# Folding the Fourier branch of an encoder block onto the symmetric half of its rows and columns

## The chip, the core and the metric

The kernel runs on one core of one Trainium2 chip. The metric is device microseconds (us) of one execution. The core has a matrix engine (TensorE, in the profile PE, its weight loads PEld), VectorE (DVE), ScalarE (ACT) and GpSimd (POOL). SyncE (SP) issues most DMA transfers; POOL issues some. Each engine works through its own instructions in program order, and they meet by semaphores.

## What is computed

One hybrid encoder layer, applied to two inputs, `prompt` and `sample`, of 2048 rows by 1024 columns each, with the same weights. One combined projection gives attention's q, k, v and gate `ga`, and the Fourier branch's input `f` (512 columns, 8 groups of 64) and gate `gf`. Cut to what matters:

```python
def _fourier_branch(f, w_fmix):
    B, S, _ = f.shape
    fg = f.reshape(B, S, N_FGROUPS, FGROUP_DIM).astype(jnp.float32)
    ff = jnp.real(jnp.fft.fft2(fg, axes=(1, 3), norm="ortho")).astype(f.dtype)
    fm = jnp.einsum('bsgc,gcd->bsgd', ff, w_fmix)
    return fm.reshape(B, S, F_WIDTH)

def _layer(h, p, g_norm, w_in, g_q, g_k, w_fmix, w_out, g_ple, w_ple_gate, w_ple):
    u = _rmsnorm(h, g_norm)
    z = u @ w_in
    q, k, v, ga, f, gf = jnp.split(z, [int(c) for c in cuts], axis=-1)
    ...
    q = _apply_axial_rope(_rmsnorm(q, g_q), cos, sin)
    k = _apply_axial_rope(_rmsnorm(k, g_k), cos, sin)
    a = _blocked_gqa(q, k, v) * jax.nn.silu(ga)
    fo = _fourier_branch(f, w_fmix) * jax.nn.silu(gf)
    h = h + jnp.concatenate([a, fo], axis=-1) @ w_out
    gate = jax.nn.sigmoid(_rmsnorm(h, g_ple) @ w_ple_gate)
    return h + (p @ w_ple) * gate
```

The branch takes the real part of a two-dimensional Fourier transform of `f`, over all 2048 rows and over the 64 columns of each group, and then multiplies each group by its own 64x64 matrix.

## The kernel before

**Tiles.** Each input is cut into 16 tiles of 128 rows; two tiles make a chunk, so there are 16 chunks, 8 (c = 0 to 7) for each input. Matrix products keep f32 accuracy by splitting both sides into an f16 value and an f16 remainder; `SPLIT3` names the three products of four that are summed. So a product over 1024 inputs takes 24 matmuls (8 slices by 3).

**Order of rows.** `token_order` sorts the rows so that tile t holds rows t, t+16, t+32 and so on (and for t > 8 the same in reverse). The transform over 2048 rows is then a first transform inside one tile, a multiplication by phase factors, and a second transform over 16 tiles. The factors are folded into the constants `c_dft2`.

**Start.** `weights` (L293) prepares the weights of the projection block by block in the order kv, q, f, gf, ga. Each block is 8 tiles of 128 rows. A tile is loaded on SP (L304), DVE takes its largest magnitude (L312), POOL reduces that over partitions (`p_mm`, L322, a PARTITION_ALL_REDUCE), DVE makes a power of two of it (L272 to L279), and ACT and DVE write the two f16 parts (L334, L335). `load` runs ahead of the block that is worked on, as far as buffers allow.

**Projection.** `project` (L566) has an iteration for each chunk. PE makes q, k and v of the chunk (`mm_q`, `mm_kv`; all projection matmuls are recorded at L451), then the sweep of the chunk before (`sweep_f` L915, `sweep_ga` L945): for each of two tiles 24 matmuls of 512 columns for `f` and as many for `gf`, after each gf the first transform of the tile (`first`, one f32 matmul, L925), and four times 24 matmuls of 256 columns for `ga`. POOL's queue stores the results to DRAM (`gd` L928, `gfd` L942, `agd` L960). Beside it, `norm_q` and its helpers normalise and rotate q and k (POOL L589 to L719, DVE, ACT) and transpose them by DMA on SP (L745, L748). `sweep_part(us)` interleaves a sweep by estimated microseconds with the code of the next iteration. Every fifth step of a sweep also advances a generator of background work (later weights, `channel_map`), and `ahead`, which starts the first scores of attention.

**Fourier, second part.** `fourier2` (L990) works through 16 blocks, 8 for each input. A block takes two loads of `gd` (`g_in`), 8 f32 matmuls of 128 columns (L1085), and a mix by `bd` (L1041, 8 matmuls). `bd` is made by `channel_map` (L501), kept in DRAM (`bdd`) and loaded at L1067. In the blocks with t = 0 and 8 a correction `fx` is added (L1101, L1043). From here on `attention` (L1124) sets the pace; `interleave` (L1662) puts `fourier2` and then `outp` (L1359) between its groups of scores, by estimates, with FILL the estimated length of that filler.

## Time and profile before

| what | us |
|---|---|
| median of 3 runs | 2667.2 (2664.6 to 2668.03) |
| profiled execution | 2670.38 |
| its span, first to last instruction | 2668.6 |
| PE busy | 2600.4 (97%) |
| POOL busy | 1773.2 (66%) |
| DVE busy | 1629.1 (61%) |
| ACT busy | 1186.0 (44%) |

The mean granted clock of TensorE was 0.994 of full speed. Busy time is time in which an instruction was being executed. In a row of the timeline the first number is the start, the second the length; `out<-in` names the tiles; brackets hold the idle time before and what ended it ("issue": the engine waited for nothing that the profile shows). A run of alike instructions is one row with its count (an f32 matmul leaves two records).

### The profile page before, as it was taken

Reading aid. Unit: us, or ns where it says so; the run is one execution under the profiler, and the core shown is the slowest. Engines: PE = TensorE matmul, PEld = TensorE weight load, DVE = VectorE, ACT = ScalarE, POOL = GpSimd, SP = SyncE. Lnnn points to the kernel's source line nnn. Section 1 sums busy time; section 2 is a strip of 40 time slices with the busy share of each in tenths; the row PEclk is TensorE's granted clock in tenths of the full one; section 3 lists DMA queues with packets and bytes.
Section 4 is the critical chain, followed back from the end, with each engine's and each line's share of the span. In section 5 each row is a group of like instructions: output and inputs, shape, how many; then the busy total and the mean of one; then the engine's idle time right before and its main releaser. Section 6 shows DMA issues by size and latency. Waiting matters only on the chain. (4 is left out here: it accounts for less than half of the span.)

```text
span 2668.6 us, 50160 instructions
## 1 busy us (share of the span) xinstructions
PE 2600.4 (97%) x20096; PEld 1393.3 (52%) x20096; DVE 1629.1 (61%) x2300; ACT 1186.0 (44%) x1983; POOL 1773.2 (66%) x1505
## 2 busy tenths in 40 slices
PE   6999999999999999999999999999999999999998
PEld 3565655655556654545455544444444544454443
DVE  6756465565555775566675666666665666656634
ACT  4443243433224553554444554544544544444442
POOL 1233242333336996888888888888888888888870
PEclk9999999999999999999999999999999999999999
DMA  8567576676528773222222224322232322232233
GB/s 251 146 165 199 170 210 179 174 186 153 146 67 254 232 215 85 63 66 66 74 72 62 66 62 96 101 68 72 64 87 63 76 75 75 63 84 75 64 76 73
DMA packets 453386, 305.38 MB, mean 114 GB/s; under 512 B 294272, under 2 KB 394816, under 8 KB 453152
## 3 DMA queue, kind: packets, MB, share of 16 engines
q1 hardware_dynamic: 440240, 260.41, 37.9%
q0 software_dynamic: 12912, 41.77, 4.3%
q8 instruction: 157, 2.57, 0.4%
q14 instruction: 77, 0.63, 0.1%
HBM read 149.50 MB, written 86.51 MB: 88 GB/s over the span
## 5 line engine op out<-in xcount | busy, mean ns | idle before, releaser
L1174 POOL TENSOR_TENSOR acc<-acc,p 128x1024 f32<-128x1024 f32 x384 | 934.8, 2434 | 118.2 <-ACT p L1169 86.3
L1204 DVE TENSOR_REDUCE a_mx<-ps_m 128x1 f32<-128x1024 f32 x498 | 609.0, 1223 | 544.7 <-PE ps_m L1196 535.8
L1169 ACT ACTIVATE p<-ps_s,s_scale 128x512 f32<-128x512 f32 x1024 | 648.2, 684 | 646.2 <-PE ps_s L1166 626.0
L1487 PE MATMUL ps_g<-w_pg,hT 64*128 64x512 f16 x2784 | 493.6, 377 | 2.1 <-DVE h L1413 2.1
L1232 PE MATMUL ps_o<-p,v 128*64 128x256 f32 x4096 | 468.4, 382 | 0.0
L451 PEld LDWEIGHTS <-uc 128*128 128x128 f16 x3072 | 301.5, 98 | 312.0 <-issue 20.6
L1166 PE MATMUL ps_s<-q,k 64*128 64x512 f16 x3072 | 434.1, 378 | 5.8 <-ACT p L1169 5.6
L1232 PEld LDWEIGHTS ps_o<-p,v 128*64 128x64 f32 x4096 | 283.9, 137 | 160.5 <-issue 28.5
L1487 PEld LDWEIGHTS <-hT 64*128 64x128 f16 x2784 | 205.3, 94 | 155.6 <-issue 13.8
L1487 PE MATMUL ps_g<-w_wo,mh 64*128 64x512 f16 x1440 | 260.3, 377 | 1.2 <-DVE seen L1453 1.2
L1487 PE MATMUL ps_g<-w_wo,mT 64*128 64x512 f16 x1440 | 256.2, 376 | 0.0
L1166 PEld LDWEIGHTS <-k 64*128 64x128 f16 x3072 | 151.3, 94 | 200.7 <-issue 78.0
L1196 PE MATMUL ps_m<-k,q 64*128 64x512 f16 x996 | 200.6, 378 | 11.3 <-DVE a_mx L1204 10.9
L942 POOL DMA_DIRECT2D gfd<-gt x32 | 19.7, 616 | 224.4 <-DVE gt L970 191.3
L451 PEld LDWEIGHTS <-w_ga 128*128 128x128 f16 x1536 | 148.8, 98 | 33.4 <-issue 11.1
L1172 POOL TENSOR_TENSOR acc<-p,p 128x1024 f32<-128x1024 f32 x64 | 150.9, 2358 | 20.7 <-ACT p L1169 19.8
L1487 PEld LDWEIGHTS <-mh 64*128 64x128 f16 x1440 | 100.2, 94 | 90.7 <-issue 18.3
L1487 PEld LDWEIGHTS <-mT 64*128 64x128 f16 x1440 | 102.8, 94 | 80.3 <-issue 3.8
L1255 DVE RECIPROCAL ps_f<-ps_f 128x256 f32<-128x256 f32 x63 | 110.6, 1756 | 20.5 <-PE ps_f L1248 20.5
L960 POOL DMA_DIRECT2D agd<-gat x64 | 35.5, 555 | 109.5 <-DVE gat L970 105.3
L451 PE MATMUL ps_x<-w_f,uc 128*128 128x512 f16 x480 | 105.9, 379 | 0.0
L451 PE MATMUL ps_x<-uc,w_ga 128*128 128x256 f16 x936 | 105.5, 273 | 0.0
(328 smaller groups left out, 3307.6 us busy)
## 6 DMA issues: line engine op xcount, KB each, us to landing
q<-qTd SPq DMA_DIRECT2D x256, 64.0 KB, 2.3
ag<-agd SPq DMA_DIRECT2D x64, 256.0 KB, 3.3
out<-h POOLq DMA_DIRECT2D x31, 512.0 KB, 3.1
x<-in_x_prompt SPq DMA_DIRECT2D x16, 512.0 KB, 5.1
gfd<-gt POOLq DMA_DIRECT2D x32, 256.0 KB, 2.6
gd<-ge POOLq DMA_DIRECT2D x32, 256.0 KB, 2.9
w_st<-in_w_out SPq DMA_DIRECT2D x32, 256.0 KB, 4.0
agd<-gat POOLq DMA_DIRECT2D x64, 128.0 KB, 3.1
```

The costliest lines, as they stand in the source:

```text
L451: self.nc.tensor.matmul(ps, lhs(ia, k), rhs(ib, k), start=(i == 0), stop=(i == 3 * ks - 1))
L942: lambda t=t, gt=gt: nc.gpsimd.dma_start(self.gfd[s][t], gt[:]))
L960: nc.gpsimd.dma_start(self.agd[s][1, r * 128:(r + 1) * 128, c * n:(c + 1) * n], gt[:, :n])
L1166: nc.tensor.matmul(S[u][e][:], w[sl], q[sl].rearrange("p h q -> p (h q)"), start=j == i == 0, stop=i + 1 == len(todo), skip_group_check=True)
L1169: nc.scalar.activation(p[:, e, :], S[u][e][:], AF.Exp, scale=self.sc["s_scale"][:])
L1172: nc.gpsimd.tensor_tensor(out=ACC[u][:], in0=P[u, 0][:], in1=p[:], op=ALU.add)
L1174: nc.gpsimd.tensor_tensor(out=ACC[u][:], in0=ACC[u][:], in1=p[:], op=ALU.add)
L1196: nc.tensor.matmul(ps[c], Q[u][0][sl, h, :], kt[s, kv, half][sl, :, 0, :], start=True, stop=True)
L1204: nc.vector.reduce_max(MX[u][:, h, half, c:c + 1], x, axis=AX.X)
L1232: nc.tensor.matmul(o[64 * f:64 * f + 64], vt[s, kv, c // 8][:, c % 8, :], p[:, e, f], start=(c == 0), stop=(c == 15))
L1255: nc.vector.reciprocal(r, r)
L1487: nc.tensor.matmul(g[0][:], g[1](ia, k)[sl], g[2](ib, k)[sl], start=a, stop=z, skip_group_check=True)
```

## The change

The Fourier transform of real data over rows can be made from sums and differences of row r and its mirror row 2048 - r, and over columns from column c and its mirror 64 - c. The change uses both. The mirrored columns are handled in the weights: the host reorders the 512 f columns of `w_in` into 8 x 33 = 264 "cosine" columns and 8 x 31 = 248 "sine" columns, and `fold_cols` turns the pairs into sums and differences on the chip, with three POOL operations on each of the eight loaded tiles of the block f. The mirrored rows are handled in u: `token_order` now puts tile t and tile t + 8, its mirror, into one chunk. For the chunks with c > 0, `fold_u` adds the f16 parts of u to f32 and `fold_s` makes sum and difference of the two tiles (both on POOL), and `fold_hl` splits them again (ACT and DVE). Sums meet only cosine columns, differences only sine columns, so f takes 24 pairs of 264 and 248 columns for a chunk instead of 48 matmuls of 512. One first transform, one `ft`, one `ge` and one store to `gd` then serve a chunk. The tiles of c = 0 (two chunks) mirror into themselves: their f stays as it was, and `first` uses four matmuls of 64 outputs and one more (`gx`, stored to `gxd`).

In `fourier2` a block takes one load of `gd` (block 0 of each input also `gxd`), 3 + 2 matmuls for the second transform and 3 + 2 for the mix; the order of blocks is 1 to 7, 0, 8 to 15. `channel_map` multiplies by a loaded mask (`c_mask`) in place of a memset and copies. The second half of v is loaded at group 6 of attention, since its buffers hold the first `gd` blocks until then. FILL goes from 765 to 756.

```diff
+CHB = ((0, 0, range(3)), (0, 99, range(3, 6)), (0, EVEN - 128, range(6, 8)),
+       (1, 0, range(4)), (1, 512 - EVEN - 128, range(4, 8)))
+BLOCKS = (1, 2, 3, 4, 5, 6, 7, 0) + tuple(range(8, 16))
...
+def token_order():
+    return base_order().reshape(2, NT // 2, 128).transpose(1, 0, 2).reshape(NT, 128)
...
+    def fold_cols(self, w):
+        g = self.nc.gpsimd
+        e = w[:, :EVEN].rearrange("p (h c) -> p h c", c=33)[:, :, 1:32]
+        o = w[:, EVEN:].rearrange("p (h c) -> p h c", c=31)
+        g.tensor_tensor(out=e, in0=e, in1=o, op=ALU.add)
+        g.tensor_scalar(out=o, in0=o, scalar1=-2.0, scalar2=None, op0=ALU.mult)
+        g.tensor_tensor(out=o, in0=o, in1=e, op=ALU.add)
...
                 _, src, cols, _, _ = blocks[i // 8]
                 sl[i] = stage(i % 8, cols)
                 nc.sync.dma_start(sl[i], src[i % 8 * 128:(i % 8 + 1) * 128, :])
+                if blocks[i // 8][0] == "f":
+                    self.fold_cols(sl[i])
...
         nc.sync.dma_start(m12[:], a["c_m12"])
         nc.sync.dma_start(wf[:], a["w_fmix"].rearrange("o g c d -> c (o g) d"))
...
             yield
         for v in range(2):
...
+                nc.tensor.matmul(ps[:, sl], m12[:, 2 * v + i, :], wf[:].rearrange("c g d -> c (g d)")[:, sl],
+                                 start=True, stop=True)
+            nc.vector.tensor_tensor(out=bd[v][:], in0=ps[:], in1=bd[v][:], op=ALU.mult)
...
+        def fold_u(i, h):
+            FT[h] = P.tile([128, CH, 512], F32, name="f_t", tag="t2", bufs=1)
+            x = lambda b: U[i][:, :, b, 4 * h:4 * h + 4, :].rearrange("p t k r -> p t (k r)")
+            nc.gpsimd.tensor_tensor(out=FT[h][:], in0=x(0), in1=x(1), op=ALU.add)
+        def fold_s(i, h):
+            x = FT.pop(h)
+            FS[h] = P.tile([128, 2, 512], F32, name="f_s", tag="sq", bufs=1)
+            for y, op in enumerate((ALU.add, ALU.subtract)):
+                nc.gpsimd.tensor_tensor(out=FS[h][:, y], in0=x[:, 0], in1=x[:, 1], op=op)
+        def fold_hl(i, h):
+            if h == 0:
+                UF[i] = P.tile([128, 2, 2, 8, 128], F16, name="uf", bufs=1)
+            o = lambda b: UF[i][:, :, b, 4 * h:4 * h + 4, :].rearrange("p y k r -> p y (k r)")
+            x = FS.pop(h)
+            nc.scalar.activation(o(0), x[:], AF.Copy)
+            nc.vector.tensor_tensor(out=o(1), in0=x[:], in1=o(0), op=ALU.subtract)
+        folds = lambda i: ok(i) and steps[i][1] > 0
...
+            if folds(i):
+                sweep_part(1.5)
+                fold_u(i, 0)
+                fold_s(i, 0)
+                fold_u(i, 1)
+                sweep_part(8.0)
+                fold_hl(i, 0)
+                fold_s(i, 1)
+                sweep_part(8.0)
+                fold_hl(i, 1)
...
         sq_u(3)
         sweep_part(11.6)
         mid()
+        fold_u(1, 0)
         make_u(3, 0)
         load_x(5, 1)
         sq_u(4)
+        fold_s(1, 0)
+        fold_u(1, 1)
+        sweep_part(3.0)
+        fold_hl(1, 0)
+        fold_s(1, 1)
+        sweep_part(6.0)
+        fold_hl(1, 1)
...
+        def first():
             pf = self.bank()
-            nc.tensor.matmul(pf[:], self.dft1[:] if t % 8 else self.dft1x[:, t // 8], F.pop(tt)[:], start=True, stop=True)
+            if c:
+                nc.tensor.matmul(pf[:], self.dft1[:], F[0][:], start=True, stop=True)
+            else:
+                for y, sl in enumerate(half):
+                    for t in range(CH):
+                        nc.tensor.matmul(pf[64 * t:64 * t + 64, sl], self.dft1x[:, 2 * t + y], F[t][:, sl],
+                                         start=True, stop=True)
...
+            if c:
+                nc.gpsimd.dma_start(self.gd[s][:, c, :], ge[:])
+                return 0.86
+            for t in range(CH):
+                nc.gpsimd.dma_start(self.gd[s].rearrange("(g y i) t d -> y g i t d", g=8, y=2)[t, :, :, 0, :],
+                                    ge[64 * t:64 * t + 64])
+            px, gx = self.bank(), w2k("ge")
+            nc.tensor.matmul(px[0:64, :EVEN], self.dft1x[:, 4], F[0][:, :EVEN], start=True, stop=True)
+            nc.scalar.activation(gx[0:64, :EVEN], px[0:64, :EVEN], AF.Copy)
+            nc.gpsimd.dma_start(self.gxd[s], gx[0:64, :EVEN])
+            return 1.3
+        if c:
             ps = self.bank()
-            yield from self.mm(ps[:], lambda b, k: uc[:, tt, b, k, :], lambda b, k: W["f"][:, b, k, :])
-            F[tt] = w2k("ft")
-            nc.scalar.activation(F[tt][:], ps[:], AF.Copy, scale=self.sc["inv_f"][:])
+            uf = UF.pop(i)
+            n = 0
+            for k in range(8):
+                for ia, ib in SPLIT3:
+                    for y, sl in enumerate(half):
+                        nc.tensor.matmul(ps[:, sl], uf[:, y, ia, k, :], W["f"][:, ib, k, sl], start=n == y == 0,
+                                         stop=n == 23, skip_group_check=True)
+                    n += 1
+                yield 0.64
+            out(ps)
+        else:
+            for tt in range(CH):
+                ps = self.bank()
+                yield from self.mm(ps[:], lambda b, k: uc[:, tt, b, k, :], lambda b, k: W["f"][:, b, k, :])
+                out(ps)
         for tt in range(CH):
...
-            yield first(tt)
+            if tt == 0:
+                yield first()
...
+        for t in BLOCKS[:FP]:
...
-            if t == 0:
-                nc.sync.dma_start(self.cx[:], self.a["c_dft2x"])
+            G[t] = self.kvp.tile([128, 512], F32, name=f"g_in{t}", tag="v1", bufs=2)
+            nc.sync.dma_start(G[t][:], self.gd[0][16 * t:16 * t + 16].rearrange("r t d -> (r t) d"))
...
-                for r in range(4):
-                    o = ps[:, r * 128:(r + 1) * 128]
-                    x = fx if y else None
-                    nc.tensor.matmul(o, fT[:, r, y, :], self.bd[:, y, r, :], start=True, stop=x is None)
-                    if x is not None:
-                        nc.tensor.matmul(o, x[:, r, :], self.bd[:, 0, r, :], start=False, stop=True)
+                x = fx if y else None
+                for b, (v, _, h) in enumerate(CHB):
+                    if v == y:
+                        sl = slice(64 * h[0], 64 * h[-1] + 64)
+                        nc.tensor.matmul(ps[:, sl], fT[:, b, :], self.bd[:, y, sl], start=h[0] == 0 or x is None,
+                                         stop=x is None,
+                                         skip_group_check=True)
+                for b in range(3 if x is not None else 0):
+                    h = CHB[b][2]
+                    sl = slice(64 * h[0], 64 * h[-1] + 64)
+                    nc.tensor.matmul(ps[:, sl], x[:, b, :], self.bd[:, 0, sl], start=False, stop=b == 2,
+                                     skip_group_check=True)
...
-                for r in range(4):
-                    nc.tensor.matmul(ps[:, r * 128:(r + 1) * 128], g[i][:, r * 128:(r + 1) * 128], c[:, i, :],
-                                     start=True, stop=True)
-                nc.scalar.activation(fT[:, :, :, 64 * i:64 * i + 64], ps[:].rearrange("p (r y d) -> p r y d", r=4, y=2),
+                bs = [b for b in range(5) if CHB[b][0] == i]
+                for j, b in enumerate(bs):
+                    o, e = ps[:, j * 128:(j + 1) * 128], EVEN * i + CHB[b][1]
+                    last = gx is None or i > 0
+                    nc.tensor.matmul(o, g[:, e:e + 128], c[:, i, :], start=True, stop=last)
+                    if not last:
+                        nc.tensor.matmul(o, gx[0:64, e:e + 128], self.cx[0:64, 1], start=False, stop=True)
...
+            if g == 6:
+                load_v(0, 1)
...
+    w = src["w_in"][..., 1280:1792].reshape(*src["w_in"].shape[:-1], 8, 64)
+    parts = [w[..., :33].reshape(*w.shape[:-2], EVEN), w[..., :32:-1].reshape(*w.shape[:-2], 512 - EVEN)]
+    src["w_in"] = np.concatenate([src["w_in"][..., :1280], *parts, src["w_in"][..., 1792:]], -1)
```

Three places show what moves. Rows have the line, the operation and the tiles; an ISA row with `p_mm` is the reduction over partitions, and one without names stands where POOL changes between it and ordinary operations. First, POOL in `weights`, before (the reductions of kv, q, f, gf and ga in a row, then the first stores of the sweep):

```order
L322 ISA
L322 ISA p_mm<-w_m_186 128x1
L322 ISA p_mm<-w_m_297 128x1
L322 ISA p_mm<-w_m_420 128x1
L322 ISA p_mm<-w_m_614 128x1
L322 ISA p_mm<-w_m_706 128x1
L942 DMA gfd<-gt 128x512
L928 DMA gd<-ge 128x512
```

And with the change, from the reduction of kv to the fold of the first f tile (`w_st` are the f tiles):

```order
L359 ISA p_mm<-w_m_185 128x1
L324 ISA
L324 TENSOR_TENSOR w_st<-w_st 128x8x31
L325 TENSOR_SCALAR w_st<-w_st 128x248
L326 TENSOR_TENSOR w_st<-w_st 128x248
```

After it the next seven tiles follow in the same way, and behind the last of them:

```order
L325 TENSOR_SCALAR w_st<-w_st 128x248
L326 TENSOR_TENSOR w_st<-w_st 128x248
L359 ISA
L359 ISA p_mm<-w_m_320 128x1
L359 ISA p_mm<-w_m_443 128x1
```

All of the fold's 24 operations now stand between the reduction of kv and that of q.

Second, POOL where the sweep of chunk 0 ends and that of chunk 1 begins, before (stores, then `norm_q(0)`):

```order
L942 DMA gfd<-gt 128x512
L928 DMA gd<-ge 128x512
L589 ISA
L589 TENSOR_TENSOR rt<-rt,g_q_t 128x256
L589 TENSOR_TENSOR rt<-rt,g_k_t 128x256
L691 TENSOR_TENSOR qn<-z,q_rs 128x1280
L696 TENSOR_TENSOR t_978<-qn,rt 128x2x512
L696 TENSOR_TENSOR t_978<-qn,rt 128x2x128
L960 DMA agd<-gat 128x256 x4
L713 TENSOR_TENSOR t_978<-t_978,t_1119 128x1280
L719 COPY kd<-t_978 128x256
L942 DMA gfd<-gt 128x512
```

And with the change (`f_t` is the sum of the two f16 parts, `f_s` sum and difference of the tiles):

```order
L1052 DMA gfd<-gt 128x512
L811 ISA
L811 TENSOR_TENSOR f_t<-uc 128x1024
L627 TENSOR_TENSOR rt<-rt,g_q_t 128x256
L627 TENSOR_TENSOR rt<-rt,g_k_t 128x256
L729 TENSOR_TENSOR qn<-z,q_rs 128x1280
L734 TENSOR_TENSOR t_1013<-qn,rt 128x2x512
L734 TENSOR_TENSOR t_1013<-qn,rt 128x2x128
L817 TENSOR_TENSOR f_s<-f_t 128x512 x2
L811 TENSOR_TENSOR f_t<-uc 128x1024
L1071 DMA agd<-gat 128x256
L817 TENSOR_TENSOR f_s<-f_t 128x512 x2
```

The folds of chunk 1 stand around `norm_q(0)`, the second half's behind it.

Third, SP at the end of the projection, before (transposes and stores of q and k of the last chunks, `mr` a transpose for the first scores, then the load of `bd`):

```order
L745 DMA_TRANSPOSE qT<-qs 128x8x128 x2
L748 DMA_TRANSPOSE kT<-ks 128x6x128
L1220 DMA_TRANSPOSE mr<-nm 128x4x128
L1152 DMA q_0_8269<-qTd 64x512 x2
L1152 DMA q_0_8270<-qTd 64x512 x2
L982 DMA c_0_8279<-in_c_dft 128x256
L986 DMA g_in_8281<-gd 128x512
```

And with the change:

```order
L783 DMA_TRANSPOSE qT<-qs 128x8x128 x2
L786 DMA_TRANSPOSE kT<-ks 128x6x128
L1349 DMA_TRANSPOSE mr<-nm 128x4x128
L784 DMA qTd<-qT 128x1024 x2
L788 DMA kTd<-kT 128x2x384
L783 DMA_TRANSPOSE qT<-qs 128x8x128 x2
L786 DMA_TRANSPOSE kT<-ks 128x6x128
L784 DMA qTd<-qT 128x1024 x2
L788 DMA kTd<-kT 128x2x384
L1184 DMA bd<-bdd 128x1024
```

`mr` now stands behind the transposes of the chunk before the last, where it stood ahead of them and of the first loads of `c` and `g_in`; `bd` still comes behind the last stores of q and k.

More of the change, by code (lines that the diff above doesn't have):

```diff
@@ L30 @@
 CAP = 5.0
-FILL = 765.0
+FILL = 756.0
 AHEAD = 14
@@ L458, in load_dft1x @@
     def load_dft1x(self, pool, dma):
[L460 to L462 removed]
+        self.dft1x = pool.tile([128, 5, 64], F32, name="dft1x", bufs=1)
+        dma(self.dft1x[:], self.a["c_dft1"][1:6, :, :64].rearrange("v p c -> p v c"))
     def setup(self, tmp):
```

203 lines of the change are left out of this document (115 added, 88 removed).

## The prediction, made before the run

> **What bounds the kernel now.** First view: the busy time of each engine by stretches of the span. Columns: length, then busy us (and instructions) of PE, PEld, DVE, ACT, POOL, the granted clock of TensorE, the DMA share, GB/s.
>
> ```profile
> 0.00:66.00 66.00, 39.41 (x210) 22.03 (x211) 45.93 (x122) 29.41 (x53) 6.99 (x18) 0.95 0.86 251
> 100.00:800.00 700.00, 700.00 (x4179) 411.43 (x4178) 402.09 (x920) 242.18 (x433) 243.82 (x237) 1.00 0.62 166
> 800.00:860.00 60.00, 54.62 (x405) 37.50 (x404) 31.67 (x47) 25.66 (x44) 37.59 (x29) 0.94 0.88 249
> 1000.00:2600.00 1600.00, 1581.05 (x13767) 791.02 (x13764) 986.66 (x915) 776.87 (x1275) 1347.77 (x1134) 1.00 0.28 73
> ```
>
> From 100 to 800 us, the projection of chunks 1 to 15, PE is busy for all of 700.00 us at full clock; in the attention stage for 98.8%. So what leaves PE there leaves the time, unless a new wait takes its place. POOL has 65% of 100 to 800 free, and 16% of the attention stage. PE's gaps lie at the start and around 830 us. Second view: PE's timeline in one chunk (start, length, line, tiles, count of records, in brackets the idle time before; ends are modelled, so I go from start to start).
>
> ```profile
> 301.23 10.52 PE L451 MATMUL ps_g<-w_f,uc 128*128 128x512 f16 x48
> 311.59 5.34 PE L451 MATMUL ps_f<-w_gf,uc 128*128 128x512 f16 x24
> 316.77 1.02 PE L925 MATMUL ps_x<-ft,dft 128*128 128x512 f32 x2
> 317.62 5.34 PE L451 MATMUL ps_x<-w_gf,uc 128*128 128x512 f16 x24
> 323.66 5.40 PE L451 MATMUL ps_x<-uc,w_ga 128*128 128x256 f16 x48
> 328.90 5.40 PE L451 MATMUL ps_g<-uc,w_ga 128*128 128x256 f16 x48
> ...
> 349.74 2.54 PE L451 MATMUL ps_x<-w_f,uc 128*128 128x512 f16 x11
> ```
>
> **What leaves PE.** A chunk takes 349.74 - 301.23 = 48.5 us, and its f projection 311.59 - 301.23 = 10.36 us. The folded one has 24 pairs of 264 and 248 columns. The nearest row is 48 matmuls of 256 columns, 328.90 - 323.66 = 5.24 us with a weight load each. Saved: 5.12 us in each of 14 folded chunks (the two chunks with c = 0 keep theirs), **-71.7 us**; down to -60 if a pair with unequal halves costs a sixth more than that row. The first DFT is 317.62 - 316.77 = 0.85 us; one goes in each of 14 chunks, **-12.0**. With c = 0 its two matmuls become two pairs in half-width columns of the array plus a short one. Whether such pairs run side by side, the row of ps_o says:
>
> ```profile
> L1232 PE MATMUL ps_o<-p,v 128*64 128x256 f32 x4096 | 468.4, 382 | 0.0
> 821.20 1.16 PE L1085 MATMUL ps_f<-c,g_in 128*128 128x128 f32 x8
> 822.19 1.06 PE L1085 MATMUL ps_g<-c,g_in 128*128 128x128 f32 x8
> 832.49 0.79 PE L1041 MATMUL ps_g<-bd,fT 128*128 128x128 f32 x2 [5.32 <-DMA bd<-bdd]
> 833.07 0.64 PE L1043 MATMUL ps_g<-bd,fx 128*128 128x128 f32 x2
> ```
>
> A record of 256 columns costs 468.4 / 4096 = 0.114 us there; the DFT's rate gives 0.85 / 4 = 0.21. They do run side by side, so c = 0 gains 0.4 us each, **-0.9** for two (+0.9 if they don't). In the second DFT four f32 matmuls of 128 columns take 822.19 - 821.20 = 0.99 us, 0.2475 each. Three of eight go in each of 16 blocks, -11.9; the mix keeps its columns in five matmuls instead of eight, by my estimate -0.1 a block, and block 0 gains about 0.5 us twice: **-12.5**. Removed: **-97.1 us**.
>
> **Added 1: folding the f weights at the start.**
>
> ```profile
> 22.05 7.33 SPq L304 DMA_DIRECT2D w_st<-in_w_in  x8
> w_st<-in_w_in SPq DMA_DIRECT2D x8, 256.0 KB, 7.4
> 27.67 0.35 POOL L322 PARTITION_ALL_REDUCE p_mm<-w_m  x1 [11.02 <-DVE n_ms L619]
> 32.77 0.15 DVE L272 TENSOR_SCALAR p_p<-p_mm 128x1 f32<-128x1 f32 x1
> 34.36 0.59 PE L451 MATMUL ps_x<-wr_q,uc 128*128 128x512 f16 x1 [7.32 <-ACT wr_q L334]
> 334.17 0.38 POOL L370 PARTITION_ALL_REDUCE p_mm<-w_m  x1 [5.93 <-issue]
> 346.87 0.72 POOL L589 TENSOR_TENSOR rt<-rt,g_q_t 128x256 f32<-128x256 f32 x1 [8.33 <-issue]
> 118.58 0.40 POOL L719 COPY kd<-t 128x256 f32<-128x256 f32 x1
> ```
>
> Before, POOL reduces wq's maximum at 27.67, DVE takes it up at 32.77, and PE, which has nothing else, starts wq's matmuls at 34.36. In the new order the 24 fold operations stand ahead of that reduction on POOL, and each waits for its f tile. The tiles are issued from 22.05 on and land some 7.4 us after issue, so folding starts near 29.4. A tile costs two two-input operations of 248 columns (0.72, the row of 346.87) and one of one input (nearest row COPY, 0.40): 1.85; eight make 14.8, to 44.2. Then POOL goes from ordinary operations back to the reduction. Where the trace shows that change, POOL stands for nothing that the profile names: 5.93 us one way, 8.33 the other. The earlier change towards folding (8.33) falls in the 11.02 us that POOL idles ahead of 27.67. So the reduction ends near 50.2, where DVE took it up at 32.77, and everything behind shifts: **+17.4**. It is 11 if this change costs nothing, 24 if the folds run at half speed for a part beside DVE; I take the rows alone.
>
> The Trainium skill ("GPSIMD Engine Reference", Instruction dispatch) says that the first call of a freshly loaded POOL kernel pays about 6 us that no instruction shows. The rows with 5.93 and 8.33 agree; with its 6 us the term would be 17.4 too, by an estimate.
>
> **Added 2: the first folded chunk.**
>
> ```profile
> 95.83 0.54 POOL L928 DMA_DIRECT2D gd<-ge  x1
> 104.31 0.72 POOL L589 TENSOR_TENSOR rt<-rt,g_q_t 128x256 f32<-128x256 f32 x1 [7.94 <-DVE q_rs L632]
> 105.11 1.59 POOL L589 TENSOR_TENSOR rt<-rt,g_k_t 128x256 f32<-128x256 f32 x1
> 113.22 2.36 POOL L960 DMA_DIRECT2D agd<-gat  x4
> 107.16 9.01 PE L451 MATMUL ps_g<-w_f,uc 128*128 128x512 f16 x41
> L1174 POOL TENSOR_TENSOR acc<-acc,p 128x1024 f32<-128x1024 f32 x384 | 934.8, 2434 | 118.2 <-ACT p L1169 86.3
> 779.40 1.05 ACT L725 ACTIVATE qs<-t 128x1024 f16<-128x1024 f32 x1
> 344.41 1.22 DVE L741 TENSOR_TENSOR qs<-t,qs 128x1024 f16<-128x1024 f32 x1
> ```
>
> Chunk 1's folds run just before PE wants them. On the clock of before: POOL's stores end near 97 (one more of them now), the change back to ordinary operations ends near 104.9 (7.94 us, as in the row), fold_u takes 2.43 (the acc row has its shape), to 107.3. Then norm_q(0) stands in between on POOL, 113.22 - 104.31 = 8.9 us, to 116.2; two adds of 512 columns, 1.3 each with some contention, to 118.8; ACT 1.05 and DVE 1.22, to 121.1. PE wants them at 106.9 (107.16 less the shorter DFT). It runs the first half's pairs and waits again: fold_u(1,1) to 121.2, a store, fold_s to 124.4, ACT and DVE to 126.7, last pairs to 129.3. Without a wait they would end at 112.1: **+17.2**. Bounds: 8 if the change back is already paid before the stores end, 22 if each two-input operation is at the slow rate of the row at 105.11 (1.59 against 0.72).
>
> **Added 3: the end of the projection.**
>
> ```profile
> 786.57 1.46 PE L451 MATMUL ps_x<-w_f,uc 128*128 128x512 f16 x6
> 828.22 0.32 SPq L1067 DMA_DIRECT2D bd<-bdd  x1
> ```
>
> PE waits 5.32 us at the first mix for bd, which SP issues at 828.22 behind the transposes and stores of the last tiles' q and k. That chain starts when PE leaves the last q and kv (786.57) and is one of latencies on SP, ACT, DVE and POOL; the change doesn't shorten it. PE comes 5.1 + 0.85 us sooner from chunk 15 and 8 x 0.2475 = 2.0 sooner from the second DFT (eight matmuls instead of sixteen before the first mix), and gives it back: **+8.0** (0 if the chain moves up too, 13 if the mr transpose, now behind three others on SP, holds it).
>
> **Added 4: folds in the other chunks.** POOL is busy for 243.82 / 700 of a chunk of 48.5 us, 16.9 us. Two adds of 1024 columns and four of 512 add 9.7 us at the lone rate, 13.6 at a factor of 1.4 (my choice between 1 and the 2.2 of the row at 105.11), so POOL has some 30 us of a new chunk of 48.5 - 5.1 - 0.9 = 42.5, and 44 in the chunks in which it also changes to a reduction and back. ACT and DVE get 2.1 and 2.4 us more. Folded rows are wanted one iteration after they are made, by my estimate near 20 us later (the matmuls that the program puts between), and eight PSUM banks give PE slack: hidden, but not everywhere, **+2** (0 to 15; nothing below, since PE has no idle there to win back; without that cover a chunk would wait for all of its 13.6 us of folds). The library changes of the folds fall where rt's stood. At nothing: channel_map's mask, which lies beside the projection's matmuls, the fewer stores and loads (PE waits for no transfer from 100 to 800 us), FILL, which goes down with the filler's own matmuls, and the later load of the second v, six groups of scores ahead of its first use; its cost with that cover gone is one transfer, 7.4 us by the row of w_st.
>
> Sum: -97.1 + 17.4 + 17.2 + 8.0 + 2.0 = -52.5. The profiled execution took 2670.4 us (span 2668.6); 2617.9. The median of the runs is 3.2 us below it: **2615 us**.
>
> **Rivals.**
> - *Both stalls are small* (A): POOL reaches the reduction and chunk 1's folds in time, since the change of library overlaps the wait for data. For it: POOL's idle 11.02 and 7.94. Against: the order of the instructions on POOL. Both gone: 2667.2 - 97.1 + 10 = 2580; one gone: 2597.
> - *Folds are dear* (B): pairs at 264/248 a sixth slower (+12), steady waits of 15 instead of 2, 2640; with both stalls at their high ends 2651. The row of ps_x<-uc,w_ga speaks against the first.
> - *POOL becomes the bound* (C, slower): a folded chunk then takes as long as POOL needs. To undo 52.5 us over 14 chunks it must lose 3.75 us more in each, a chunk of 46.3: POOL would need 29.4 us of folds above its 16.9, three times the lone rate. It decides from 42.5 us on. For it: 1.59 against 0.72 in the row at 105.11, a factor of 2.2 beside DVE; with that factor folds are 21 us and POOL has 38, below the bound; with reductions in the chunk it is above. At a factor of 3.3, which no row shows, POOL has 16.9 + 32 = 48.9 us, 6.4 over, and 14 chunks bring 2615 + 90 = 2705.
> - *The folded f doesn't shorten PE* (D): if a pair took as long as two 512-column matmuls, for the weight loads, 97.1 - 71.7 = 25.4 would go, and 44.6 - 5.1 = 39.5 come: 2681. The w_ga row excludes nearly all of it.
>
> For C, the Trainium skill ("GPSIMD Engine Reference", Elementwise and Key points) speaks against the change: two-input elementwise work is about twice as slow on POOL as on VectorE and shares its SBUF interface with it. The rows agree: 2434 ns against DVE's 1.22 us for 1024 columns, and 1.59 against 0.72. By that rule the folds cost POOL 21 us, not 9.7; it still fits.
>
> **Numbers.** Forecast 0.69, A 0.14, B 0.11, C 0.04, D 0.02. The range takes in A and all but the end of B: 2580 to 2648. A measurement of this kernel can tell 0.2%, 5.3 us, from no change. Faster 0.93; same 0.03; slower 0.04.
>
> **What would show it.** Right: w_f matmuls at 5.24 us a chunk; DVE's p_p for wq near 50, not 32.77; a wait of PE near 14 us before the first folded matmul, ended by the folds' DVE operation; a wait for bd near 13 us; no PE idle from chunk 2 to 14. Wrong: PE idle in every chunk behind folds (C), or p_p still near 33 (A).

## The result and the profile after

| | before | after |
|---|---|---|
| median, us | 2667.5 (4 runs, 2664.6 to 2668.0) | 2729.2 (4 runs, 2728.7 to 2735.1) |
| ratio, 95% interval | 1 | 1.0239 (1.0221 to 1.0256) |
| profiled execution (span), us | 2670.4 (2668.6) | 2728.7 (2726.9) |
| PE busy, us | 2600.4 | 2536.3 |
| granted clock | 0.994 | 0.974 |

The changed kernel is 2.4% slower: 114 us above the 2615 that was predicted, and outside the range. PE has 64 us less to do and yet ends 58 us later. The windows of after, with the columns of those of before (length, busy us of PE, PEld, DVE, ACT, POOL, granted clock, DMA share, GB/s):

```profile
100.00:800.00 700.00, 627.56 (x4067) 403.39 (x4064) 511.02 (x944) 247.78 (x433) 356.28 (x296) 0.94 0.61 160
...
1000.00:2600.00 1600.00, 1558.52 (x13555) 776.03 (x13553) 991.91 (x926) 769.31 (x1266) 1344.71 (x1116) 1.00 0.29 73
```

In the projection PE was busy for all of 700 us; now 72 us of it are gaps, and the clock is granted at 0.94. POOL is at 356 of 700, far from full. DVE has risen by 109 us, though the change gave it only 2.4 us a chunk.

The span difference by stages (f(i) is the start of PE's f matmuls of chunk i, in the order of work; attention's first accumulation is POOL's first `acc<-p,p`, at 825.4 us in before and 869.1 in after):

| stage | before | after | difference | by the prediction's terms |
|---|---|---|---|---|
| start to f(2) | 155.7 | 185.7 | +30.0 | +28.2 |
| f(2) to f(15) | 630.9 | 637.4 | +6.5 | -70.0 |
| f(15) to attention's first accumulation | 38.8 | 46.0 | +7.2 | 0 |
| first accumulation to the end | 1843.2 | 1857.8 | +14.6 | -10.5 |

(To f(2): Added 1 and 2 less what one folded chunk and one with c = 0 save; f(2) to f(15): 12 folded chunks of 5.97 and the 0.4 of c = 0, less Added 4. In the third row Added 3's loss meets what chunk 15 and the first blocks save.) The first stage came as forecast. The second is 76.5 us off, the third 7.2 and the last 25.

First, what PE does without a wait in between. The timeline of PE in after, in chunk 2 and at the second transform (start, length, line, tiles, count of records):

```profile
185.67 5.40 PE L1036 MATMUL ps_x<-w_f,uf 128*128 128x264 f16 x48
190.91 5.34 PE L488 MATMUL ps_x<-w_gf,uc 128*128 128x512 f16 x24
196.09 1.02 PE L1009 MATMUL ps_x<-ft,dft 128*128 128x512 f32 x2
...
864.88 0.94 PE L1207 MATMUL ps_g<-c,g_in 128*128 128x128 f32 x6
865.65 0.61 PE L1207 MATMUL ps_f<-c,g_in 128*128 128x128 f32 x4
866.10 0.83 PE L1207 MATMUL ps_g<-c,g_in 128*128 128x128 f32 x6
```

The 48 folded matmuls take 190.91 - 185.67 = 5.24 us, as forecast, and the second transform's halves 0.77 and 0.45 instead of 0.99 each. So the large terms of "What leaves PE" did leave it.

The start, POOL with the fold of the first tile and the reduction of wq, then DVE's use of it and PE's first wq matmul (brackets: idle time before, and what ended it):

```profile
28.79 0.67 POOL L324 TENSOR_TENSOR w_st<-w_st 128x248 f32<-128x248 f32 x1 [12.95 <-DMA w_st<-in_w_in]
29.56 0.88 POOL L325 TENSOR_SCALAR w_st<-w_st 128x248 f32<-128x248 f32 x1
...
53.23 0.38 POOL L359 PARTITION_ALL_REDUCE p_mm<-w_m  x1 [5.98 <-issue]
53.65 0.15 DVE L298 TENSOR_SCALAR p_p<-p_mm 128x1 f32<-128x1 f32 x1 [20.64 <-POOL p_mm L359]
55.25 0.58 PE L488 MATMUL ps_x<-wr_q,uc 128*128 128x512 f16 x1 [29.48 <-ACT wr_q L371]
```

The folds run from 28.79 to 47.26 (18.5 us), POOL needs 5.98 for the change, and wq is late by 55.25 - 34.36 = 20.9 us.

The waits of PE in the projection of after (waited for: us in total, times, longest), and the first folded chunk's two:

```profile
PE ps_f L1009 <- ACT ft L1004: 16.5, 3, 7.2
PE ps_g L1009 <- ACT ft L1004: 15.5, 1, 15.5
PE ps_g L1036 <- ACT uf L824: 11.2, 1, 11.2
PE ps_x L1325 <- DMA q<-qTd: 10.7, 1, 10.7
PE ps_x L1009 <- ACT ft L1004: 9.1, 2, 5.9
PE ps_x L1325 <- DVE a_mx L1333: 6.7, 1, 6.7
```

```profile
139.00 1.03 PE L1036 MATMUL ps_g<-w_f,uf 128*128 128x264 f16 x4 [11.23 <-ACT uf L824]
141.20 4.02 PE L1036 MATMUL ps_g<-w_f,uf 128*128 128x264 f16 x18 [1.16 <-DVE uf L825]
```

PE waits for folded rows (uf) only in chunk 1. From chunk 2 on the folds are always there in time. What is late is `ft`, ACT's copy of f out of PSUM (where PE leaves its products) ahead of the first transform: six waits, 41 us. The chunks show it: 42.5 us (the forecast length) four times between f(2) and f(15), and 47.4 to 60.9 in the other nine (one of them, 48.4, is the chunk with c = 0). From f(2) to f(15) these six waits and those for q and `a_mx` make 58.4 us; the stage is 78.5 us longer than its 558.9 with all folds hidden, and the other 20 go with matmuls that run slower behind a wait (the mean granted clock from 150 to 750 is 0.95; one such place follows).

One such wait, followed back. The timeline of before, then of after, DVE, SP, ACT and PE around the start of a chunk's f (301.2 in before, 323.7 in after). `hl` is the split of the next u, `uc` its transpose, `x` the load of the next rows, `jk` their squares.

```profile
287.84 2.47 DVE L649 SCALAR_TENSOR_TENSOR hl<-x,rsq_z,hl 128x1024 f16<-128x1024 f32 x2
289.18 5.63 SPq L444 DMA_TRANSPOSE uc<-hl  x2
294.86 1.20 SPq L595 DMA_DIRECT2D x<-in_x_sample  x2
299.51 1.06 ACT L602 ACTIVATE jk<-x 128x1024 f16<-128x1024 f32 x1 [4.40 <-DMA x<-in_x_sample]
306.61 0.69 ACT L935 ACTIVATE ft<-ps_g,inv_f 128x512 f32<-128x512 f32 x1 [3.82 <-PE ps_g L451]
```

```profile
324.99 3.98 DVE L687 SCALAR_TENSOR_TENSOR hl<-x,rsq_z,hl 128x1024 f16<-128x1024 f32 x2
327.44 4.99 SPq L481 DMA_TRANSPOSE uc<-hl  x2
332.48 1.07 SPq L633 DMA_DIRECT2D x<-in_x_sample  x2
336.71 1.06 ACT L640 ACTIVATE jk<-x 128x1024 f16<-128x1024 f32 x1 [11.13 <-DMA x<-in_x_sample]
339.86 0.70 ACT L1004 ACTIVATE ft<-ps_g,inv_f 128x512 f32<-128x512 f32 x1
340.61 2.08 PE L1009 MATMUL ps_f<-ft,dft 128*128 128x512 f32 x2 [6.35 <-ACT ft L1004]
```

Before, `hl` ended 11 us ahead of f; after, 5 us behind it. The transposes wait for `hl`, the load of x stands behind them on SP, ACT's `jk` waits 11.13 us for that load, and `ft`, whose data PE finished at 328.9, stands behind `jk` on ACT. Before, ACT waited for PE at `ft`; now PE waits for ACT. The first transform after the gap takes 1.87 us to the next row (342.48) instead of 0.85: the granted clock is 0.50 from 340.6 to 342.5, 0.57 up to 344.3 and 1.00 from there to 350.

Part of DVE's lateness is this (timeline of DVE and POOL in after; the 128x22 rows are steps of the square root for norms):

```profile
152.22 0.17 DVE L271 TENSOR_SCALAR rsq_hx<-n_ms 128x22 f32<-128x22 f32 x1
152.34 2.06 DVE L274 TENSOR_TENSOR rsq_t<-rsq_y 128x22 f32<-128x22 f32 x1
152.24 2.12 POOL L811 TENSOR_TENSOR f_t<-uc 128x1024 f32<-128x1024 f16 x1
```

A two-input operation of 22 columns, 0.18 us elsewhere, starts beside POOL's fold and ends with it: 152.34 + 2.06 = 154.40 against 154.36. The one-input row ahead of it starts 0.02 us before the fold and takes its usual 0.17. One-input rows aren't free of such holding: `ks` (L776, a CAST of 256 columns) took 2.32 us at 331.47, beside POOL's rotation, and 0.29 in before (294.76).

Five of the six waits for `ft` stand behind ACT's wait for x, as this one does. The longest stands behind another:

```profile
593.25 0.91 ACT L468 ACTIVATE p_hl<-p_in,p_f 128x256 f16<-128x256 f32 x2 [15.57 <-DVE p_f L463]
594.78 2.08 PE L1009 MATMUL ps_g<-ft,dft 128*128 128x512 f32 x2 [15.49 <-ACT ft L1004]
```

Here ACT's queue stands for DVE's `p_f` (the background split of the input p), and DVE comes to it only after the same steps of the square root, four of which take 6.36 us together in place of 0.72 beside POOL's folds from 583.75 to 590.71.

### The profile page after: what moved, and what is told of

Read it like the earlier page. It is cut to its first block, busy times and chain, and to the rows that moved or that the text cites. A ratio compares the mean times of both kernels' runs of the same rounds, so it can differ in the third digit from the quotient of the medians.

```text
span 2726.9 us, 49881 instructions
## 1 busy us (share of the span) xinstructions
PE 2536.3 (93%) x19896; PEld 1377.5 (51%) x19896; DVE 1745.7 (64%) x2326; ACT 1182.6 (43%) x1983; POOL 1920.6 (70%) x1598
## 5 line engine op out<-in xcount | busy, mean ns | idle before, releaser
L488 PEld LDWEIGHTS <-uc 128*128 128x128 f16 x2400 | 239.8, 100 | 267.3 <-issue 64.0
L1619 PE MATMUL ps_g<-w_wo,mh 64*128 64x512 f16 x1440 | 260.0, 376 | 13.7 <-DVE mh L1529 12.4
L488 PE MATMUL ps_x<-w_gf,uc 128*128 128x512 f16 x552 | 135.0, 404 | 0.0
L488 PE MATMUL ps_x<-wr_q,uc 128*128 128x512 f16 x384 | 88.0, 387 | 29.7 <-ACT wr_q L371 29.5
L488 PE MATMUL ps_x<-uc,w_ga 128*128 128x256 f16 x1008 | 113.5, 273 | 0.0
```

The lines of the kernel that those rows point to most:

```text
L488: self.nc.tensor.matmul(ps, lhs(ia, k), rhs(ib, k), start=(i == 0), stop=(i == 3 * ks - 1))
L1619: nc.tensor.matmul(g[0][:], g[1](ia, k)[sl], g[2](ib, k)[sl], start=a, stop=z, skip_group_check=True)
```

## The experiments

A single time is one run; where three rounds were made, the interval is given. Differences are to the changed kernel's 2729.2 unless said otherwise; runs of before on the same chips gave 2663 to 2671.

**Do the row folds cost it, and on which engine?** First without them: `uf` is filled from the unfolded u by the same ACT and DVE operations, so the Fourier branch is computed from rows that were never summed.

```diff
-            nc.gpsimd.tensor_tensor(out=FT[h][:], in0=x(0), in1=x(1), op=ALU.add)
-                nc.gpsimd.tensor_tensor(out=FS[h][:, y], in0=x[:, 0], in1=x[:, 1], op=op)
-            nc.scalar.activation(o(0), x[:], AF.Copy)
-            nc.vector.tensor_tensor(out=o(1), in0=x[:], in1=o(0), op=ALU.subtract)
+            nc.scalar.activation(o(0), x(0), AF.Copy)
+            nc.vector.tensor_tensor(out=o(1), in0=x(1), in1=o(0), op=ALU.subtract)
```

> The changed kernel without the fold of the rows on POOL: fold_u and fold_s are left out, ACT and DVE fill uf from the unfolded u, so f is not that of the reference. Everything else is as in the changed kernel. Theory P: with POOL's adds gone DVE's Newton steps (128x22, 0.18 us, now up to 2.06 us) are short again, a chunk's period is 42.5 us, the waits of 58 us from 150 to 800 us and the half clock behind them go, and chunk 1's wait of 12 us: 2635 to 2655 us. Theory L: DVE's steps are short, but PE still waits for ft behind the x load in most chunks: 2685 to 2710 us.

Measured: 2649.9, 79 us less. Then the same six adds per chunk on DVE, in the same places:

```diff
-            nc.gpsimd.tensor_tensor(out=FT[h][:], in0=x(0), in1=x(1), op=ALU.add)
+            nc.vector.tensor_tensor(out=FT[h][:], in0=x(0), in1=x(1), op=ALU.add)
-                nc.gpsimd.tensor_tensor(out=FS[h][:, y], in0=x[:, 0], in1=x[:, 1], op=op)
+                nc.vector.tensor_tensor(out=FS[h][:, y], in0=x[:, 0], in1=x[:, 1], op=op)
```

> All six adds of the row fold on DVE in place of POOL. The run without them took 2650 us with chunks of 42.5 us. Theory H (what hurts is POOL: DVE's two-input steps stand while a POOL add runs, and POOL's stores queue behind fold_s): Newton's steps are 0.18 us again, chunks 42.5 to 44 us, chunk 1 waits less; DVE has some 5 us more in a chunk: 2645 to 2670 us. Rival D (any 5 to 10 us more in the chain of a chunk are too much, on whichever engine): chunks of 46 us or more, 2690 to 2730 us.

Measured: 2659.2, 70 us less with all of the work done. f(2) to f(15) takes 564.6 us without the folds and 573.1 with them on DVE, against 637.4 on POOL and 558.9 forecast. The windows from 150 to 750 us, of after, of no folds and of folds on DVE:

```profile
150.00:750.00 600.00, 548.22 (x3572) 354.52 (x3570) 443.58 (x778) 213.98 (x377) 309.58 (x256) 0.95 0.63 166
```

```profile
150.00:750.00 600.00, 596.83 (x4022) 393.89 (x4021) 395.35 (x864) 233.03 (x408) 216.47 (x207) 1.00 0.67 179
```

```profile
150.00:750.00 600.00, 590.71 (x3946) 387.01 (x3944) 468.33 (x941) 232.10 (x404) 210.35 (x201) 0.99 0.68 179
```

DVE takes over all of the folds for 25 us more busy time (468 against 444), and in the same 600 us the kernel gets further (3946 matmuls against 3572). So where the adds run decides, and PE is nearly full again.

**Is PE's saving on the path at all in after?** Every pair is made twice, into the same result: 5.24 us more for PE in each of 14 chunks, 73 us.

```diff
-            for k in range(8):
+            for k in range(16):
+                n = k % 8 * 3
```

> The 24 pairs of the folded f are made twice into the same bank (the second pass overwrites the first), so PE has 5.2 us more in each of 14 chunks, as many matmul columns for f as before the change; nothing else differs. If a chain of waits sets the chunk's period in the changed kernel (47 to 48 us on the mean) and PE's saving is off the path, the waits shrink by what is added: 2730 to 2755 us, with less PE idle. If PE's work is on the path: 2729 + 73 = 2802 us.

Measured: 2739.4, +10 for 73 us of added matmuls. With the folds on POOL the chunk isn't PE's; of what was saved on PE in f, some 10 us at most reach the time. (Part of the added work fills what had been slow matmuls: the granted clock from 150 to 750 rises from 0.95 to 0.99.)

**Which link of the chain?** Three tries to loosen it with the folds left on POOL. (a) The squares of x three chunks ahead (`sq_u`, the `jk` rows) moved behind the sweep, out of `ft`'s way:

```diff
-            if ok(i + 3):
-                sq_u(i + 3)
...
+            if ok(i + 3):
+                sq_u(i + 3)
```

> The changed kernel took 2729 us; in the projection PE stood five times (7.2, 6.4, 5.9, 2.9, 3.2 us) before the first DFT for ACT's ft, and ACT stood before that for the load of x that it squares. Here the squares of x stand behind the sweep on ACT. Theory L (the x load at the head of ACT's queue holds back z and ft, and the halved f leaves PE too little work to cover it): those five waits go, 25.5 us and the slow matmuls behind them (10 to 20 us), so 2685 to 2700 us. Theory P (POOL's folds, and DVE which is held while they run, are late as a whole; x is only the last to come): the waits turn up at another ACT instruction, 2715 to 2735 us.

Measured: 2722.3; PE still waits 39.8 us for `ft`. (b) The folds issued some 11 us later:

```diff
-                sweep_part(1.5)
+                sweep_part(13.0)
-                sweep_part(8.0)
+                sweep_part(6.0)
-                sweep_part(8.0)
+                sweep_part(4.0)
```

> The row fold stays on POOL but is issued 11 us of matmuls later in the iteration, so behind the stores of gf and the first DFT, when Newton's steps on DVE are over. Theory H, holding part (the place of the adds beside Newton's ten DVE steps costs about 6 us of DVE chain in a chunk): steps at 0.18 us, chunks 42.5 to 45 us, 2655 to 2680 us. Rival T (POOL's time and its queue as a whole, wherever the adds stand): 2700 us or more.

Measured: 2732.9. (c) The first half's adds at their old place, its split `fold_hl` 7 us later and the second half's at the end of the sweep (the second half's `fold_s` moves back with the first split):

```diff
-                sweep_part(8.0)
+                sweep_part(15.0)
                 fold_hl(i, 0)
                 fold_s(i, 1)
-                sweep_part(8.0)
+                sweep_part(1000.0)
                 fold_hl(i, 1)
```

> The changed kernel with the row folds on POOL at their old place, but ACT's and DVE's split (fold_hl) issued later: 15 us of matmuls behind the adds instead of 8, the second half at the end of the sweep. Theory Q (ACT's copy to uf waits for POOL at the head of ACT's queue, 32 us in the projection, with z, ft and th behind it): ACT's wait for f_s goes below 10 us, and the waits of PE for ft fall by more than half: 2685 to 2710 us. Rival T (POOL's time is too much wherever it is waited for): 2720 us or more, with the wait at another place.

Measured: 2730.9. What ACT waited for from 150 to 760 us, in after, in (a) and in (b):

```profile
ACT jk L640 <- DMA x<-in_x_sample: 61.0, 8, 11.1
...
ACT uf L824 <- POOL f_s L817: 32.0, 8, 10.2
```

```profile
ACT vs L717 <- DMA vd<-vs: 60.2, 10, 14.7
...
ACT z L715 <- POOL qn L729: 38.5, 7, 11.0
```

```profile
ACT uf L824 <- POOL f_s L817: 80.5, 16, 15.0
ACT jk L640 <- DMA x<-in_x_sample: 57.9, 8, 8.2
```

With the squares late, ACT's wait for x is gone and it waits as long for the store of v (also behind the transposes on SP) and for POOL; with the folds late, it waits for the folds. In (b) the 128x22 rows of DVE take 0.18 us again, and it is no faster: the holding of these rows isn't the cause by itself either. Other rows of DVE are held in their place (`kd`, L775, takes 2.1 us there, 1.7 in after and 0.85 without the folds), but its busy time from 150 to 750 falls to 398, near the 395 without folds. In (c) ACT's wait for `f_s` falls only from 32.0 to 25.0, so that this link was hardly loosened, and PE keeps six waits of 3.2 to 15.6 us for `ft`. Shown is that the adds on POOL do it and that neither (a) nor (b) alone undoes it; that the loop through the queues of POOL, ACT, DVE and SP as a whole is the mechanism is how I read these rows.

**The start.** The weight folds stay on POOL but come after the reductions of kv and q (`fold_cols` in the loop over the tiles of block f):

```diff
-                if blocks[i // 8][0] == "f":
-                    self.fold_cols(sl[i])
...
+                if name == "f":
+                    self.fold_cols(sl[8 * b + k])
```

> The fold of the f weights stands behind the reduction of q's maximum on POOL. Both theories: the first wq matmul, at 55.25 us in the changed kernel, is back near 34.4, and what follows moves up with it unless the f weights come late (folds from about 36 to 51, reduction near 57, PE wants f at 62): 2708 to 2715 us. If the startup's loss is caught up anyway by the waits behind it: 2725 or more.

Measured: 2724.7, only 4.5 less. wq starts at 33.5 and f(0) at 67.7 (84.1 in after), but the lateness moves on: PE waits 5.9 for w_f and 4.1 for w_gf, and 11.7 for chunk 1's rows. f(2) is at 179.5. With rows and weights folded on DVE (the weights behind q's reduction, two operations a tile, where `scalar_tensor_tensor` makes o = e - 2o in one), and chunk 1's folds ahead of `norm_q(0)`:

```diff
+        v.tensor_tensor(out=e, in0=e, in1=o, op=ALU.add)
+        v.scalar_tensor_tensor(out=o, in0=o, scalar=-2.0, in1=e, op0=ALU.mult, op1=ALU.add)
...
+        for h in range(2):
+            fold_u(1, h)
+            fold_s(1, h)
+            fold_hl(1, h)
```

> The row folds on DVE as in the run that took 2659 us, and the two startup losses undone: the f weights are folded on DVE (two operations a tile) behind the reduction of q's maximum, and chunk 1's folds stand ahead of the scales and of norm_q(0). Theory: wq's first matmul back near 34.4 (56.4 there), f of chunk 0 at 62 to 68 us (85.2), chunk 1's f without the wait of 8.4 us, and nothing else moves: 2659 - 17 to 22 - 9 = 2628 to 2635 us. Rival: what is won at the start is lost again because the later weights come no sooner (gf and ga): 2640 to 2655 us.

Measured: 2647.7; f(0) at 61.5, f(2) at 167.1. The start's stall is gone and so is the wait for chunk 1's rows, but PE now waits 5.1 us for `ge` ahead of the next q and 6.9 for chunk 1's `ft`.

**Attention.** It lasts 1857.8 us from the first accumulation in after, 1843.2 in before, with 7 us less for PE to do. PE's waits from then on, in after:

```profile
PE ps_s L1295 <- ACT p L1298: 15.6, 37, 1.7
PE ps_m L1325 <- DVE a_mx L1333: 14.4, 21, 2.6
PE ps_g L1619 <- DVE mh L1529: 12.4, 10, 2.4
```

And in before:

```profile
PE ps_s L1166 <- ACT p L1169: 7.5, 20, 2.0
```

In before the wait for `mh` (the input of `outp`'s matmuls) doesn't occur, and p costs 7.5. Six things were tried. FILL alone back to 765:

> FILL back to 765. From the first accumulation of attention to the last the changed kernel takes 18 us more than before although PE has 4 us less to do there. Theory: the pace of the filler is why (out-projection work comes before its inputs), and with 765 this is 0 to 5 us again: 2710 to 2717 us. Rival: the pace has nothing to do with it: within 5 us of 2729.

Measured: 2735.4; the stage takes 1867.4. Three of five second-transform matmuls a block made twice (8 as in before, the same result):

> Three of a block's five matmuls of the second DFT are made twice (in 14 blocks of 16 and in part of the two others), so PE has 8 instead of 5 there again, 11 us more in all. If the matmuls that the change takes from the second DFT were on the path: 2740 us. If POOL and ACT set the pace of attention while the second DFT runs, and they were not: 2725 to 2732 us.

Measured: 2733.7; stage 1865.7. Both together:

> The changed kernel with 8 matmuls a block in the second DFT (three made twice) and FILL 765, so that attention has as much filler and the same pace as before the change. From the first accumulation to the end the kernel before took 1843 us with 39 us of PE idle, the changed one 1858 with 61, though PE has 7 us less to do. Theory F (the pace and the amount of filler no longer fit each other): 1843 to 1850 us with 40 to 45 us idle. Theory O (the order of tiles, blocks and loads that the change brings makes the new waits): 1862 to 1875 us with 55 to 65 us idle.

Measured: 2740.2; stage 1865.9. Block 0 third instead of eighth (on top of the version with the start on DVE, 2647.7):

> As the run before it on this chip, with block 0 of the second DFT as the third block in place of the eighth. In the changed kernel attention and the rest behind it take 15 us more than before from the first accumulation to the end, where 12 us less were forecast. Theory B0: the out-projection's first tiles need block 0, which now comes last of its half, and PE waits for their inputs: 8 to 15 us less than the run before it. Rival: the order of blocks is not why: within 4 us of it.

Measured: 2646.6. The kernel before, with v's second half loaded at group 6:

> The kernel before with one part of the change: the second half of v is loaded at group 6 of attention. If this late load is what costs attention 15 us: 1855 to 1860 us from the first accumulation to the end, 2680 in all. If not: 1843 and 2667, within 4 us.

Measured: 2668.4, stage 1842.4. FILL 748 on the version with the start on DVE:

> As the first run of this call, with FILL 748 in place of 756. 765 cost the changed kernel 6 us. If the pace of the filler explains the loss in attention: 5 to 10 us less than the first run of this call. If 756 already fits the work that is left: the same to 6 us more.

Measured: 2656.0; the accumulations end earlier than without that edit (2545 against 2564), and the tail behind them is 109 us instead of 82. None of the six accounts for the 15 us. Left was the length that a filler step announces to `interleave`: the change had lowered it with the number of matmuls. With 8 matmuls and FILL 765, as in the third run, and before's announced lengths as the only further edit:

```diff
-                yield 0.215 * len(bs)
+                yield 0.86
...
-                yield 0.64
+                yield 0.86
```

> The changed kernel, with its second DFT padded back to 8 matmuls a block (three of five are made twice, into the same result), its two filler steps announced with before's estimate (0.86 us each) and FILL back at 765. Filler work and pace between the groups of scores are then those of before, and what is left of the change in the attention stage is the order of blocks, tiles and loads. If the changed pace is what lengthens that stage, it takes 1843 us again from the first accumulation to the end (before 1843.2, changed 1857.9; PE idle 39.0 and 60.7), and the run about 2715. If not, it takes 1862 or more (the 11 us of added matmuls come on top, as in the run with the doubled matmuls, 1865.7), and the run is near 2735.

Measured: 2703.9, ratio 1.0141 (1.0124 to 1.0158); the stage takes 1833.3, 32.6 less than without that edit. That is also 10 us below the 1843 of before, which neither theory had; what wins these 10 isn't shown.

**Together.** Both folds on DVE, chunk 1 left at its place; and the same with the squares late:

> Both folds on DVE, the one of the f weights behind the reduction of q's maximum, and chunk 1's folds at the place of the change. Moving chunk 1's folds ahead of norm_q(0) won its wait and lost 5 to 7 us behind it (chunk 2 began 105.6 us after chunk 0 there and 98.2 us in the run with only the row folds on DVE). Theory: the start's gain without that loss, 2638 to 2645 us, ratio 0.989 to 0.992. Rival (the loss came from the sooner start itself): 2648 or more.

> As the run before it, and the squares of x behind the sweep on ACT. With the folds off POOL, ACT's wait for x (72 us in the projection) is the longest that stands ahead of ft; PE still stands about 6 us for ft. If it is the cause of these: 4 to 8 us less than the run before it; if another wait takes its place, within 3 us.

Measured: 2652.4, ratio 0.9941 (0.9925 to 0.9958), and 2653.3, 0.9954 (0.9939 to 0.9969): faster than before by 0.6%, and the squares make no difference. Last, the first of the two with before's announced lengths and FILL 765, and the five matmuls a block that the change has:

> The changed kernel with both folds (rows of u and f weights) on VectorE and with the announced filler lengths of before (0.86 us for each step of the second transform, FILL 765), but without the doubled matmuls. If the announced lengths are what lengthens the attention stage, whatever PE's work in it, the stage takes 1820 to 1835 us from the first accumulation to the end (1859.6 with the folds on VectorE alone, 1833.3 with the pace of before and 8 matmuls a block), and the run comes to 2617 to 2630. If announced lengths must match the real ones, the pace that fitted 8 matmuls a block fits 5 no longer, the stage stays near 1860 and the run near 2652.

Measured: 2618.0 (2614.8 to 2619.3), ratio 0.9809 (0.9793 to 0.9826): 1.9% faster than before. Its stage takes 1829.8 (1859.6 with the change's own lengths and FILL 756). PE's waits there, then the first and last start of `outp`'s matmuls by `mh`, in this version, in after and in before:

```profile
PE ps_m L1324 <- DVE a_mx L1332: 13.0, 21, 1.6
PE ps_s L1294 <- ACT p L1297: 5.3, 19, 0.6
...
L1618 PE MATMUL ps_g<-w_wo,mh x1440: 372/376/631, 950.0 to 2525.5; 64*128 64x512 f16 x180
```

```profile
L1619 PE MATMUL ps_g<-w_wo,mh x1440: 372/376/387, 1018.6 to 2635.0; 64*128 64x512 f16 x180
```

```profile
L1487 PE MATMUL ps_g<-w_wo,mh x1440: 372/376/631, 1001.1 to 2577.7; 64*128 64x512 f16 x180
```

The waits for `mh` and most of those for p are gone. `outp` begins 950.0 - 786.4 = 163.6 us after the first accumulation, in after 1018.6 - 869.1 = 149.5, in before 1001.1 - 825.4 = 175.7: with shorter announced lengths it runs closer behind the results that it needs. That this earlier start is what makes the waits is read from these rows; a run with `outp` alone shifted wasn't made.

## Why the prediction was wrong, point by point

- **What bounds the kernel now**: right for before (PE had no gap), and the conclusion had its condition, "unless a new wait takes its place". The waits did.
- **What leaves PE** (-97.1): right in the rows shown. That the last version, with folds on DVE and the pace of before, comes to 2618.0 against a forecast of 2615 is luck and doesn't bear the sum out: there the weights' fold has left the path of wq (f(2) comes 9.1 us later than before and not 28.2), f(2) to f(15) saves 53.5 and not 70.0, the third stage loses 5.4 and not 0, and the last saves 13.4 and not 10.5.
- **Added 1** (+17.4): right in mechanism and place, measured +20.9. Mis-sized was the one-input operation, taken from a COPY row at 0.40; it takes 0.83 to 0.88, so a tile costs 2.3 us and not 1.85. The change to the reduction took 5.98, as the row of 5.93 said; the row of 8.33, which the prediction also sets beside a figure of 6 us, is more than a third above it.
- **Added 2** (+17.2): right in place and nearly in size, 15.4 us by the rows (the pairs end at 148.38; without a wait they would have at 139.00 - 11.23 + 5.24 = 133.01). The two waits, 11.2 + 1.2 = 12.4 us, are both for the first half's `uf`, ACT's and then DVE's part, where 14.2 was forecast. The second wait that the prediction describes, for the second half's rows, didn't come: what it was to cost went into matmuls at a granted clock of 0.50 (139 to 145 us). Up to f(2) the terms are off by 1.8 us in all; Added 1 came out too low and Added 2 too high, so part of that is luck.
- **Added 3** (+8.0): the wait named is not the one that came. PE waits 3.24 us for `bd`, not 13, since it loses time ahead of it, to the first scores that `ahead` puts into the projection:

```profile
836.73 1.10 PE L1009 MATMUL ps_x<-ft,dft 128*128 128x512 f32 x2 [2.65 <-DVE a_mx L1333]
846.10 1.18 PE L1325 MATMUL ps_x<-k,q 64*128 64x512 f16 x2 [6.33 <-DVE a_mx L1333]
```

These two waits stand between f(15) and the first accumulation, which takes 46.0 us where 38.8 were forecast. It takes 45.1 without any row fold too, and 38.2 with the pairs doubled, so by these runs it is the shorter f that runs into `a_mx`, on whichever engine the folds are.
- **Added 4** (+2, 0 to 15): **the step that failed**, by 76.5 us. Its price for the folds was even too high: f_t 2.13 us and f_s 1.27 make 2 x 2.13 + 4 x 1.27 = 9.3 us a chunk, not 13.6. Wrong was the cover. I weighed POOL's busy share against the length of a chunk, and asked only whether folded rows are there when PE wants them; from chunk 2 on they are. In place of 2 us the stage lost 78.5, and 64.3 of these come back when the same adds run on DVE (637.4 to 573.1). What the folds delay, as I read the rows, is the other work in the same queues: POOL's stores and rotation, ACT's and DVE's splits, through them `hl`, the transposes, the loads on SP and the copies that PE needs. In the chunk shown of before that chain had 11 us in hand ahead of f. "Nothing below, since PE has no idle there" was true; "eight PSUM banks give PE slack" was not, because the first transform stands in PE's own order right behind its `ft`.
- **FILL "at nothing"**, with the -12.5 of the second transform: the second step that failed, by 25 us. The prediction weighed FILL alone and has no term for the lengths that `fourier2` announces, which the change had lowered with it (0.86 a step to 0.215 a matmul). FILL and the announced lengths aren't bookkeeping; with them the start of `outp` moves. Announcing as before, with FILL 765, brings -29.8 (1859.6 to 1829.8), and the stage then saves 13.4 against before, 10.5 by the terms.
- **Rivals**: the sign was that of C, but not by its condition. POOL is busy for 309.58 of 600 us, some 25 us of a mean chunk of 49.0, far below the 42.5 from which C was to decide. What the prediction names beside it, POOL and DVE slowing each other, did show in the rows (2.06 us against 0.18). A is out by the rows of the start and the 12.4 us, D and the first half of B by the 5.24 us; B's steady waits were there, but they cost 78.5 us and not 15.

The Trainium skill ("GPSIMD Engine Reference", Engine selection) sends elementwise additions of two inputs to VectorE, as about twice as slow on GpSimd. The runs agree: f_t takes 2.13 us on POOL and 1.22 on DVE, and the move is worth 70 us. The prediction weighed that rule as a price only, and the price was on the high side (13.6 us a chunk for 9.3).

## What to carry to other kernels

Work for an engine with half of its time free need not be hidden: what stands behind it in its queue and in the queues that it feeds can come late. Measure the lead of that chain (11 us from `hl` to f in the chunk shown), not the engine's busy share alone, and try the work on another engine. Where the bound engine is relieved, doubling its saved work again is a cheap test of whether the saving is on the path. If an interleaver goes by announced lengths, treat a change of them as a change of the program, and time it apart from the change that it came with.

## What the runs showed of the hardware

- A DVE operation with two inputs of 22 columns (0.18 us) that starts beside a POOL operation of two inputs ended with it, after 2.06 us; median 2.06 over 19 of the steps that read `rsq_y` in after, and 0.18 with the folds on DVE. So 9.3 us of POOL work a chunk also raised DVE's busy time: 395 us from 150 to 750 without the folds, 444 with them on POOL, 468 with all of them on DVE. The Trainium skill ("GPSIMD Engine Reference", Key points) names contention with DVE instructions that have two SBUF inputs; the rows agree and give its size.
- On POOL a one-input operation by a constant (0.83 us for 248 columns) was slower than a two-input one of the same size (0.67).
- After a gap of 6.35 us PE's first transform took 1.87 us and not 0.85, at a granted clock of 0.50, so that a wait costs more than its length: from f(2) to f(15) 58.4 us of waits went with 78.5 us lost.
